# Block 1 of a two-block model on one core: wide gating products, a queued half of the output projection, key scaling on another engine, and a norm's matmul moved

## The chip, the cores and the metric

The kernel runs on one core of a Trainium2 chip. The metric is the device time of one execution in microseconds. Of the kernel before three runs are shown; their median is 2776.11 us. The engines are named as in the profile: PE is TensorE, PEld its weight loads, DVE is VectorE, ACT is ScalarE, POOL is GpSimd, SP is SyncE.

## The reference

One sequence of 512 tokens with 1024 features goes through two blocks of two layers each. The change lies in the mixers of the first block and in the norm ahead of the second. A layer of the first block is, cut to what matters:

```python
h = _rms_norm(x, in_norm_g[l])
y = h @ w_in[l] + b_in[l]
(mq, mk, mv, mo, mi, mf, hq, hf, hi, hg, sq, sk, sv) = _split_cols(y, IN_SPLITS)
qk = jax.nn.silu(_causal_conv(jnp.concatenate([mq, mk], axis=-1), ...))
m_h = mlstm_chunkwise(q, k, v, mi, mf + mlstm_f_bias[l])          # 4 heads
m_out = _head_rms_norm(m_h, mlstm_norm_g[l], 4) * sigmoid(mo)
h_h = hgrn2_chunkwise(hq, hf, hi, lb_all[l])                      # 4 heads
h_out = _head_rms_norm(h_h, hgrn_norm_g[l], 4) * silu(hg)
s_out = swa_sink_attention(q_s, k_s, v_s, swa_sinks[l])           # 8 heads
x = x + concatenate([m_out, h_out, s_out]) @ w_out[l]
u = _rms_norm(x, mlp_norm_g[l]) @ w_up[l]
x = x + square(relu(u)) @ w_down[l]
x = x + sigmoid(_rms_norm(x, ...) @ w_ple_gate[l]) * e
```

A layer of the second block first forms `mod = silu(c) @ w_mod + b_mod`, six vectors of shifts, scales and gates, and then runs three kinds of attention and a gated MLP with a short convolution. Everything is float32.

## The kernel before

The activations `x` stay in SBUF as eight tiles of 128 features by 512 tokens. Each product of float32 matrices is made of three matmuls: both factors are split into a high part (a cast on ACT, L136) and a low part (a difference on DVE, L137), and `mm3` (L176 to L178) multiplies high by high, high by low and low by high into one PSUM tile. Weights stream from HBM through SP's queue in pieces of 512 KB and are split in the same way (`wh`, `wl`). `feat_group` and `tok_group` run such products for a group of output tiles and hand each finished PSUM tile to a sink.

The mixers of a layer of block 1 are written in this order. First comes the attention with sinks (`swa`). Then `hgrn` and `mlstm`, two generators, are stepped alternately. `hgrn` goes over eight levels of a binary split of the tokens: at a level with half length h (64, 32, ... 1) it subtracts the log decays around the middle (L710, L711), takes the exponential on ACT (L715), multiplies the second halves by the queries (L718) and the first halves by the keys (L719), both on DVE and both over 128x256 elements, and runs 64x64 score matmuls (L731), whose results DVE copies into place under a mask (L742). There are two tiles a level and seven levels with products: 14 key scalings a layer. `mlstm` forms its gates and a running maximum M, sends M from POOL's queue through DRAM (L809) so that each head can read it back spread over the partitions (L850, also on POOL's queue; POOL then masks it, L852), and convolves its queries and keys on DVE (L834, L839). Each of its four heads makes four score matmuls (L858), exponentials of M on ACT (L861, L863), four products on DVE (L865), ten value matmuls (L870) and a copy to `nS` (L872).

The gates `gg` (for HGRN's output) and `gm` (for mLSTM's) come from two projections. Then follow the output projection's three parts: the attention's rows (`w_oa1`, two groups of 48 matmuls of 512 columns), HGRN's rows (`w_oh1`) and mLSTM's rows (`w_ob1`, in two halves of 256 columns). `hgrn_out` multiplies `gg` by HGRN's output and its norm factor, 16 operations of 128x64 (L779); `mlstm_out` does the same for `gm` (L896) after a norm of its own. Both are transposed on PE (L518) before their parts of the projection, and the sink adds each PSUM tile to `x` on DVE (L498).

That is the order in the source. The order in which the instructions stand on the engines is set by a scheduler, which lists all of them by priorities and a timeline of its own; the order written in the source sets the priorities. Each engine then works in order. A norm (`norm_stats`) is a list of steps that `start` begins and `tick` continues: after a number of columns of matmuls, given by the table `PAUSES` by the running number of the norm, its next step is put into the program, where the matmuls that sum the squares (L260) and the one that spreads the factor (L267) are steps. Norm 17 is that of the second half of the tokens at the entry of block 2. The eight chunks of block 1's MLP (`up`, `down`) take along the products for the second block's modulation (`mod_part`, L1034), six a chunk.

```python
    def tick(self, work):
        if self.pend:
            self.pend[0][1] += work
            if self.pend[0][1] >= self.pend[0][2]:
                self.step()
```

## Time and profile before

| what | value |
|---|---|
| median of three runs | 2776.11 us (2770.52 to 2781.68) |
| the profiled execution's own time | 2770.02 us |
| its span | 2768.2 us |
| mean granted clock of TensorE | 0.989 of full |
| busy: PE, DVE, ACT, POOL | 2691.5, 1782.7, 1182.1, 233.0 us |
| mixers of block 1, first and second layer | to about 283 us; about 703 to 985 us |
| block 2 begins | about 1430 us |

The profile is one execution. Its time is 1.8 us above its span, and it stands at the lower end of the three runs. The busy shares are means over stages with different limits, so single stretches are to be read beside them. A wait names the instruction that ended an idle time of an engine; PEclk or the last but two column of a table of stretches is the granted clock of TensorE, 1.00 for 2.4 GHz and 0.5 for 1.2 GHz.

### The profile page before, as it was taken

To read this page: it belongs to the slowest core of one execution; us is meant where nothing else is said; L and a number is where in the kernel's file an instruction comes from. 1 tells how busy PE (TensorE), PEld (TensorE's weight loads), DVE (VectorE), ACT (ScalarE), POOL (GpSimd) and SP (SyncE) were. 2 spreads that over 40 slices of the span, in tenths; PEclk is the share of its full clock that TensorE was granted. 3 is DMA by queue.
4 is the path that set the end of the run, shared out by engine and by line. 5 is a ranking of instruction groups with operands and counts; after the bars stand their busy time and mean duration, and the time that the engine had idled before them with its cause. 6 is when DMAs were issued, how large, how long until landed. Compare 5 with 4: busy or idle time off the path is not lost.

```text
span 2768.2 us, 42721 instructions
## 1 busy us (share of the span) xinstructions
PE 2691.5 (97%) x16360; PEld 2287.3 (83%) x16360; DVE 1782.7 (64%) x3888; ACT 1182.1 (43%) x2340; POOL 233.0 (8%) x606
## 2 busy tenths in 40 slices
PE   8999999999999999999999999999999999999998
PEld 7876988889977788778988777888889787888887
DVE  7677777568767767765863676655554476664555
ACT  4644532326374543233543555333234455532332
POOL 2000100002200010000122300000001310000000
PEclk9999999999999999999999999999999999999999
DMA  4211487332321127843323211233332312133222
GB/s 155 77 40 54 143 266 229 111 103 92 92 73 47 55 89 238 254 156 100 107 67 110 62 57 63 84 88 101 99 94 80 118 37 78 51 103 99 88 86 78
DMA packets 87644, 285.59 MB, mean 103 GB/s; under 512 B 10972, under 2 KB 15132, under 8 KB 87440
## 3 DMA queue, kind: packets, MB, share of 16 engines
q1 hardware_dynamic: 81280, 266.49, 30.1%
q0 software_dynamic: 5872, 16.35, 2.3%
q8 instruction: 128, 2.10, 0.3%
q14 instruction: 76, 0.62, 0.1%
q10 hardware_dynamic: 288, 0.03, 0.0%
HBM read 280.69 MB, written 2.14 MB: 102 GB/s over the span
## 4 chain that ended last, share of the span: by engine, by line
PE 80%; DVE 8%; DMA 5%; ACT 3%; issue 2%; POOL 2%; SPq 0%; DVEq 0%; ACTq 0%; POOLq 0%
PE ps_mm L176 13%; PE ps_mm L177 12%; PE ps_mm L178 12%; PE ps_T L176 5%; PE ps_T L177 5%; PE ps_T L178 5%; PE ps_S L176 5%; PE ps_S L177 5%; PE ps_S L178 5%; DMA wm<-w_mod 4%; PE ps_S L1091 2%; PE ps_o L1137 1%; DVE wm L1034 1%; PE ps_T L1131 1%; PE ps_S L582 1%
## 5 line engine op out<-in xcount | busy, mean ns | idle before, releaser
L136 ACT CAST wh<-wr 128x1024 fp32r<-128x1024 f32 (+4 forms) x414 | 406.6, 986 | 659.4 <-PE ps_mm L177 209.4
L137 DVE TENSOR_TENSOR wl<-wr,wh 128x1024 fp32r<-128x1024 f32 (+4 forms) x414 | 474.8, 1148 | 306.7 <-ACT wh L136 300.2
L176 PE MATMUL ps_mm<-slotA,wh 128*128 128x512 f32 (+1 forms) x632 | 227.1, 365 | 1.8 <-ACT slotA L317 0.7
L177 PE MATMUL ps_mm<-slotA,wh 128*128 128x512 f32 (+1 forms) x632 | 225.7, 359 | 2.0 <-DVE slotA L318 2.0
L178 PE MATMUL ps_mm<-slotA,wl 128*128 128x512 f32 (+1 forms) x632 | 224.7, 357 | 0.0
L176 PE MATMUL ps_mm<-wh,slotA 128*128 128x256 f32 (+3 forms) x688 | 207.6, 303 | 1.1 <-ACT slotB L1084 1.1
L178 PE MATMUL ps_mm<-wh,slotA 128*128 128x256 f32 (+3 forms) x688 | 205.9, 299 | 0.0
L177 PE MATMUL ps_mm<-wl,slotA 128*128 128x256 f32 (+3 forms) x688 | 205.9, 300 | 0.0
L1034 DVE CUSTOM_DVE_ANT_0 wm<-wm,sc 128x1024 f32<-128x1024 f32 x96 | 117.5, 1224 | 67.6 <-DMA wm<-w_mod 66.7
L136 ACT CAST m_h<-tmp 128x512 fp32r<-128x512 f32 (+1 forms) x122 | 71.3, 587 | 208.1 <-DVE tmp L913 171.8
L176 PE MATMUL ps_mm<-slotB,wh 128*128 128x512 f32 (+1 forms) x408 | 143.8, 357 | 3.4 <-ACT slotB L136 2.6
L176 PEld LDWEIGHTS ps_mm<-wh,slotA 128*128 128x128 f32 x688 | 131.1, 191 | 14.3 <-issue 10.6
L177 PE MATMUL ps_mm<-slotB,wh 128*128 128x512 f32 (+1 forms) x408 | 141.9, 349 | 0.0
L178 PE MATMUL ps_mm<-slotB,wl 128*128 128x512 f32 (+1 forms) x408 | 140.9, 346 | 0.0
L176 PEld LDWEIGHTS ps_mm<-slotA,wh 128*128 128x128 f32 x632 | 120.5, 193 | 21.3 <-issue 3.2
L177 PEld LDWEIGHTS ps_mm<-wl,slotA 128*128 128x128 f32 x688 | 131.1, 191 | 7.9 <-issue 6.8
L177 PEld LDWEIGHTS ps_mm<-slotA,wh 128*128 128x128 f32 x632 | 120.7, 191 | 19.8 <-DVE slotA L318 2.9
L178 PEld LDWEIGHTS ps_mm<-slotA,wl 128*128 128x128 f32 x632 | 120.8, 191 | 19.3 <-issue 3.9
L178 PEld LDWEIGHTS ps_mm<-wh,slotA 128*128 128x128 f32 x688 | 131.3, 191 | 4.5 <-issue 3.2
L1107 ACT ACTIVATE at_s<-at_s,at_st 128x512 f32<-128x512 f32 (+3 forms) x160 | 89.4, 559 | 104.0 <-DVE at_st L1105 96.2
L176 PE MATMUL ps_S<-m_h,wh 128*128 128x512 f32 (+1 forms) x355 | 129.4, 365 | 0.7 <-DVE yacc L947 0.4
L178 PE MATMUL ps_S<-m_h,wl 128*128 128x512 f32 (+1 forms) x355 | 129.2, 364 | 0.0
(633 smaller groups left out, 7183.9 us busy)
## 6 DMA issues: line engine op xcount, KB each, us to landing
wr<-w_up SPq DMA_DIRECT2D x152, 512.0 KB, 3.9
wm<-w_mod SPq DMA_DIRECT2D x96, 512.0 KB, 4.6
wr<-w_dn SPq DMA_DIRECT2D x64, 512.0 KB, 3.9
wr<-w_dn SPq DMA_DIRECT2D x32, 384.0 KB, 3.1
wr<-w_dn SPq DMA_DIRECT2D x32, 320.0 KB, 2.8
wr<-w_f SPq DMA_DIRECT2D x16, 512.0 KB, 3.7
wr<-w_pg SPq DMA_DIRECT2D x16, 512.0 KB, 3.8
wr<-w_t SPq DMA_DIRECT2D x12, 512.0 KB, 4.7
```

Of the source, the lines that this page charges most:

```text
L136: nc.scalar.copy(hi, src)
L137: nc.vector.tensor_tensor(lo, src, hi.bitcast(F32), ALU.subtract)
L176: nc.tensor.matmul(out, ah, bh, start=i == 0, stop=False)
L177: nc.tensor.matmul(out, ah, bl, start=False, stop=False)
L178: m = nc.tensor.matmul(out, al, bh, start=False, stop=i == n - 1)
L582: nc.tensor.matmul(pt, qs[f][b:b + 64, tt], qs[4][b:b + 64, k0:k0 + w], start=True, stop=True)
L1034: nc.vector.tensor_tensor_reduce(w, w, self.sc, 1.0, 0.0, ALU.mult, ALU.add, accum_out=self.mod[l][:, j:j + 1])
L1091: i = nc.tensor.matmul(pts[u], q, k, start=True, stop=True, tile_position=None if row is None else (row, 0))
L1107: nc.scalar.activation(s, s, AF.Exp, bias=st[:, 0:1], scale=-1.0, accum_out=st[:, 1:2])
L1131: nc.tensor.transpose(tp[:, c * P:c * P + P], s[:, c * P:c * P + P], self.ident)
L1137: nc.tensor.matmul(po[u * 64:u * 64 + 64], v(c, u), pT[:, c * P:c * P + P], start=c == 0, stop=c == t, tile_position=(0, u * 64))
```

## The change

Five things are done, and the source is otherwise the same.

- In `hgrn_out` the norm factor is multiplied into HGRN's output over 128x512 elements by a broadcast operand, and `gg` then takes one product of 128x256 a token tile. `mlstm_out` has the same form, with one product of 128x16x64 ahead.
- The calls of `hgrn_out` and `mlstm_out` stand ahead of the output projection.
- The second group of `w_oa1`, 48 matmuls, is issued after the last score matmul of the last mLSTM head (`issue_after`).
- HGRN's key scaling runs on POOL instead of DVE.
- Norm 17 gets longer pauses, and `mod_part` is called for one column at a time from the sink of `down`.

```diff
--- before.py
+++ after.py
@@ -28,7 +28,7 @@
 
 PAUSES = {
     5: (6000, 15000), 7: (25000, 15000), 8: (9000, 6000),
-    10: (25000, 15000), 16: (18000, 15000), 20: (6000, 15000),
+    10: (25000, 15000), 16: (18000, 15000), 17: (15000, 9000), 20: (6000, 15000),
     21: (15000, 9000), 23: (9000, 6000), 24: (6000, 15000),
 }
 
@@ -493,16 +493,17 @@
                 else:
                     nc.vector.scalar_tensor_tensor(z, th, 1.0, gh[:, 0:256], ALU.add, ALU.mult)
             self.tok_group(w, 8, 256, act, gate_sink)
+        self.hgrn_out(gg)
+        self.mlstm_out(mp, sp, gm)
 
         sub = lambda y, i: [y[t][:, i * P:i * P + P] for t in range(NT)]
         sink = lambda m, pt, sl: nc.vector.tensor_tensor(self.x[m][:, sl], self.x[m][:, sl], pt, ALU.add)
         act = [self.to_feat(X, sub(ysw, i), "mm") for i in range(4)]
         for g in range(2):
-            self.feat_group(self.wload("w_oa1", l * 2 + g, 4 * 512), 4, 4, act, sink, 4 * g)
-        self.hgrn_out(gg)
+            with self.tc.issue_after(self.done["head", 3]) if g else nullcontext():
+                self.feat_group(self.wload("w_oa1", l * 2 + g, 4 * 512), 4, 4, act, sink, 4 * g)
         act = [self.to_feat(X, sub(gg, i)) for i in range(2)]
         self.feat_group(self.wload("w_oh1", l, 2 * 1024), 2, 8, act, sink)
-        self.mlstm_out(mp, sp, gm)
         ctx.close()
         act = [self.to_feat(X, sub(gm, i)) for i in range(2)]
         wo = self.wload("w_ob1", l, 2 * 1024)
@@ -716,7 +717,7 @@
                     q4 = q_[i].rearrange("p (s two h) -> p s two h", two=2, h=h)
                     k4 = k_[i].rearrange("p (s two h) -> p s two h", two=2, h=h)
                     nc.vector.tensor_tensor(d4[:, :, 1, :], d4[:, :, 1, :], q4[:, :, 1, :], ALU.mult)
-                    nc.vector.tensor_tensor(d4[:, :, 0, :], d4[:, :, 0, :], k4[:, :, 0, :], ALU.mult)
+                    nc.gpsimd.tensor_tensor(d4[:, :, 0, :], d4[:, :, 0, :], k4[:, :, 0, :], ALU.mult)
                     ops.append((dd, dd))
                 else:
                     ops.append((k_[i], q_[i]))
@@ -773,11 +774,12 @@
 
     def hgrn_out(self, gg):
         oS, r = self.hgo
+        for u in range(2):
+            o3 = oS[u].rearrange("p (a e) -> p a e", e=64)
+            self.nc.vector.tensor_tensor(o3, o3, r[:, u * 8:u * 8 + 8].unsqueeze(2).broadcast_to([P, 8, 64]), ALU.mult)
         for t in range(NT):
-            for h in range(4):
-                g, o = gg[t][:, h * 64:h * 64 + 64], (t % 2) * 256 + h * 64
-                self.nc.vector.scalar_tensor_tensor(g, oS[t // 2][:, o:o + 64], r[:, t * 4 + h:t * 4 + h + 1], g,
-                                                    ALU.mult, ALU.mult)
+            o = (t % 2) * 256
+            self.nc.vector.tensor_tensor(gg[t], oS[t // 2][:, o:o + 256], gg[t], ALU.mult)
 
 
     def mlstm(self, l, mp, sp, yf, yv, yg, fv, fb):
@@ -855,7 +857,7 @@
                 w = S - j * P
                 js = slice(j * P, j * P + P)
                 pt = self.ps("ST"[j % 2])[:, :w]
-                nc.tensor.matmul(pt, k[b:b + 64, js], q[b:b + 64, j * P:S], start=True, stop=True)
+                self.done["head", h] = nc.tensor.matmul(pt, k[b:b + 64, js], q[b:b + 64, j * P:S], start=True, stop=True).ins
                 W = sp.tile([P, S], F32, name="ml_W", tag="ml_W", bufs=2)[:, :w]
                 aj = ac[:, j * 4 + h:j * 4 + h + 1]
                 nc.scalar.activation(W[:, 0:P], Md[:, j, :], AF.Exp, bias=aj, scale=-1.0)
@@ -890,11 +892,11 @@
         rs = sp.tile([P, 16], F32, name="ml_rs")
         self.rsqrt(sp, rs, ssq, 1.0 / 64, EPS, 16, "ml")
         nc.vector.tensor_tensor(rs, rs, r, ALU.mult)
+        n3 = num[:, :, 0:64]
+        nc.vector.tensor_tensor(n3, n3, rs.unsqueeze(2).broadcast_to([P, 16, 64]), ALU.mult)
         for t in range(NT):
-            for h in range(4):
-                g = gm[t][:, h * 64:h * 64 + 64]
-                nc.vector.scalar_tensor_tensor(g, nS[:, t, h, 0:64], rs[:, t * 4 + h:t * 4 + h + 1], g,
-                                               ALU.mult, ALU.mult)
+            g3 = gm[t].rearrange("p (h e) -> p h e", e=64)
+            nc.vector.tensor_tensor(g3, nS[:, t, :, 0:64], g3, ALU.mult)
 
 
     def mlp1(self, l, fp, act, nxt):
@@ -941,6 +943,8 @@
                 if c == 7:
                     nc.vector.tensor_tensor(self.x[m][:, sl], self.x[m][:, sl], pt, ALU.add)
                     return
+                if m < 6:
+                    self.mod_part(l, fp, c * 6 + m, c * 6 + m + 1)
                 if c == 0:
                     nc.scalar.copy(yacc[m], pt)
                 else:
@@ -960,7 +964,6 @@
         self.silu_c(fp, R2)
         for c in range(1, 8):
             up(c)
-            self.mod_part(l, fp, (c - 1) * 6, c * 6)
             down(c - 1)
         pe = []
         for k in range(2):
```

What becomes of it on the engines, in the first layer. PE at the last head of mLSTM, where L858 (now L860) are the scores, L870 (L872) the values and L176 to L178 on `slotA,wh` the matmuls of `w_oa1`. Before:

```order
L858 MATMUL ps_T<-yf_1733,yf_1801 128x384
L858 MATMUL ps_S<-yf_1733,yf_1801 128x256
L176 MATMUL ps_mm<-slotA,wh 128x512
L177 MATMUL ps_mm<-slotA,wh 128x512
L178 MATMUL ps_mm<-slotA,wl 128x512
L176 MATMUL ps_mm<-slotA,wh 128x512
L177 MATMUL ps_mm<-slotA,wh 128x512
L178 MATMUL ps_mm<-slotA,wl 128x512
L858 MATMUL ps_T<-yf_1733,yf_1801 128x128
L870 MATMUL ps_T<-yv_1522,ml_P_2466 128x66 x2
```

After the change:

```order
L872 MATMUL ps_T<-yv_1525,ml_P_2442 128x66
L860 MATMUL ps_T<-yf_1733,yf_1801 128x384
L860 MATMUL ps_S<-yf_1733,yf_1801 128x256
L860 MATMUL ps_T<-yf_1733,yf_1801 128x128
L176 MATMUL ps_mm<-slotA,wh 128x512
L177 MATMUL ps_mm<-slotA,wh 128x512
L178 MATMUL ps_mm<-slotA,wl 128x512
L176 MATMUL ps_mm<-slotA,wh 128x512
L177 MATMUL ps_mm<-slotA,wh 128x512
L178 MATMUL ps_mm<-slotA,wl 128x512
```

Before, two groups of three matmuls stood among the last head's scores and none between its values and the transposes of `gg`. Now the scores stand together, 25 matmuls of `w_oa1` follow, then that head's ten values, then 23 more, then the transposes. No matmul of `w_oa1` stands between the first three heads any more; of the 96, 70 stood ahead of the second head's first score, and now 48. In the second layer 58 stood there, and now 48.

DVE at the products for `gg` (L779, now L779 and L782; `ml_r` and `ml_ssq` belong to mLSTM's norm, `hg_t` and `hg_r` to HGRN's). Before:

```order
L130 TENSOR_TENSOR hg_t<-hg_r 128x16
L888 TENSOR_TENSOR ml_ssq<-ml_ssq,ml_r 128x16
L131 TENSOR_TENSOR hg_t<-hg_t,hg_v 128x16
L889 TENSOR_TENSOR ml_ssq<-ml_ssq,ml_r 128x16
L132 SCALAR_TENSOR_TENSOR hg_r<-hg_t,hg_r 128x16
L121 TENSOR_SCALAR ml_v<-ml_ssq 128x16
L779 SCALAR_TENSOR_TENSOR gg_1518<-slotB,hg_r,gg_1518 128x64 x4
L779 SCALAR_TENSOR_TENSOR gg_1519<-slotB,hg_r,gg_1519 128x64 x4
L779 SCALAR_TENSOR_TENSOR gg_1520<-slotB,hg_r,gg_1520 128x64 x4
L779 SCALAR_TENSOR_TENSOR gg_1521<-slotB,hg_r,gg_1521 128x64 x4
```

After the change:

```order
L882 SCALAR_TENSOR_TENSOR ml_r<-ml_nS 128x16
L779 TENSOR_TENSOR slotB<-slotB,hg_r 128x512 x2
L883 TENSOR_TENSOR ml_r<-ml_r,ml_gd 128x16
L889 TENSOR_REDUCE ml_ssq<-tmp 128x8
L782 TENSOR_TENSOR gg_1518<-slotB,gg_1518 128x256
L782 TENSOR_TENSOR gg_1519<-slotB,gg_1519 128x256
L889 TENSOR_REDUCE ml_ssq<-tmp 128x8
L782 TENSOR_TENSOR gg_1520<-slotB,gg_1520 128x256
L782 TENSOR_TENSOR gg_1521<-slotB,gg_1521 128x256
L884 RECIPROCAL ml_r<-ml_r 128x16
```

The products of `gg` stood behind mLSTM's sums of squares, in 16 pieces; now there are two wide and four of a whole tile, around those sums, with the first step on `ml_nS` ahead of them.

POOL at the transfers of M, L809 and L850 before, L811 and L852 now (L852, now L854, is the mask; `brow` and the sets to zero belong to other steps). Before:

```order
L694 MEMSET slotB 128x512 x4
L696 MEMSET slotB 128x512 x2
L402 DMA brow<-row 128x256 x2
L809 DMA ml_md_1833<-ml_Md 4x512
L850 DMA slotB<-ml_md_1833 128x512 x2
L852 AFFINE_SELECT ml_Md<-slotB 128x512
L850 DMA slotB<-ml_md_1833 128x512
L852 AFFINE_SELECT ml_Md<-slotB 128x512
```

After the change:

```order
L720 TENSOR_TENSOR tmp<-tmp,slotB 128x8x32 x2
L720 TENSOR_TENSOR tmp<-tmp,slotB 128x16x16 x2
L720 TENSOR_TENSOR tmp<-tmp,slotB 128x32x8 x2
L811 DMA ml_md_1833<-ml_Md 4x512
L720 TENSOR_TENSOR tmp<-tmp,slotB 128x64x4
L852 DMA slotB<-ml_md_1833 128x512 x2
L720 TENSOR_TENSOR tmp<-tmp,slotB 128x64x4
L854 AFFINE_SELECT ml_Md<-slotB 128x512
L720 TENSOR_TENSOR tmp<-tmp,slotB 128x128x2 x2
L720 TENSOR_TENSOR tmp<-tmp,slotB 128x256 x2
L852 DMA slotB<-ml_md_1833 128x512
L854 AFFINE_SELECT ml_Md<-slotB 128x512
```

The key scalings (L720) of the first levels stand ahead of the transfer of M, those of the levels 64x4, 128x2 and 256 between and behind its two directions. In the second layer it is the same pattern.

PE at the sums of norm 17 (L260), ahead of block 2. Before 72 matmuls of 256 columns of one projection stand ahead of them and 72 between them and L267; after the change 96 and 48. The order of SP's queue is the same before and after, as is that of all engines in block 1's MLP.

## Rows read from the trace of the kernel before

**Rows 1.** The page, part 1: busy us (share of the span) xinstructions, TensorE.

```profile
PE 2691.5 (97%) x16360; PEld 2287.3 (83%) x16360; DVE 1782.7 (64%) x3888; ACT 1182.1 (43%) x2340; POOL 233.0 (8%) x606
```

**Rows 2.** Busy time by stretch: stretch and its length, then by engine, clock, DMA.

```profile
core 0: us, PE busy (x) PEld busy (x) DVE busy (x) ACT busy (x) POOL busy (x), PEclk, DMA share, GB/s
180.00:200.00 20.00, 15.86 (x230) 14.56 (x231) 19.26 (x43) 7.24 (x10) 2.15 (x4) 1.00 0.27 81
200.00:220.00 20.00, 17.44 (x224) 14.28 (x226) 19.85 (x35) 9.12 (x14) 0.13 (x1) 0.91 0.16 54
226.00:262.00 36.00, 34.98 (x194) 25.52 (x193) 20.39 (x44) 23.02 (x56) 3.64 (x6) 1.00 0.13 45
262.30:272.80 10.50, 7.07 (x18) 4.50 (x19) 10.07 (x52) 2.12 (x4) 0.00 (x0) 0.51 0.15 50
880.00:900.00 20.00, 17.35 (x238) 16.26 (x238) 19.72 (x45) 6.79 (x10) 3.62 (x4) 0.91 0.27 81
900.00:920.00 20.00, 17.67 (x257) 14.10 (x257) 17.61 (x30) 10.60 (x19) 0.00 (x0) 0.83 0.17 55
962.00:976.00 14.00, 12.49 (x46) 8.21 (x46) 13.45 (x58) 3.66 (x6) 0.56 (x1) 0.88 0.12 40
1420.00:1440.00 20.00, 15.27 (x114) 15.02 (x113) 8.55 (x30) 7.68 (x22) 4.24 (x16) 0.91 0.08 19
```

**Rows 3.** PE's waits, 178 to 210 and 883 to 909: us, times, longest.

```profile
PE ps_o L680 <- DVE hg_st L687: 1.2, 1, 1.2
PE ps_T L814 <- DVE ml_W L807: 2.1, 1, 2.1
PE ps_o L680 <- DVE hg_st L687: 2.7, 1, 2.7
PE ps_S L731 <- DVE slotA L742: 2.0, 1, 2.0
```

**Rows 4.** PE's waits, 256 to 284.

```profile
PE ps_T L518 <- DVE gg L779: 3.7, 1, 3.7
PE ps_T L870 <- DVE ml_P L865: 0.8, 1, 0.8
```

**Rows 5.** The chain in order of time, 269 to 274: start us, us, what.

```profile
271.86 0.43 PE ps_mm L177
...
272.91 0.24 PE ps_mm L177
```

**Rows 6.** PE's waits, 1419 to 1430.

```profile
PE ps_mm L260 <- DVE n_acc L256: 4.7, 1, 4.7
```

**Rows 7.** Groups of instructions, 262 to 276: busy us, mean ns | idle before.

```profile
L896 DVE SCALAR_TENSOR_TENSOR gm<-ml_nS,ml_rs,gm 128x64 f32<-128x64 f32 x16 | 3.2, 283 | 0.0
L779 DVE SCALAR_TENSOR_TENSOR gg<-slotB,hg_r,gg 128x64 f32<-128x64 f32 x16 | 3.2, 277 | 0.0
L887 DVE TENSOR_REDUCE ml_ssq<-tmp 128x8 f32<-128x512 f32 x2 | 1.3, 654 | 0.0
```

**Rows 8.** Groups of instructions, 226 to 262.

```profile
L137 DVE TENSOR_TENSOR wl<-wr,wh 128x1024 fp32r<-128x1024 f32 x3 | 3.7, 1220 | 1.7 <-ACT wh L136 1.7
...
L176 PE MATMUL ps_mm<-slotA,wh 128*128 128x512 f32 x14 | 6.1, 433 | 0.0
```

**Rows 9.** Groups of instructions, 180 to 215.

```profile
L719 DVE TENSOR_TENSOR tmp<-tmp,slotB 128x256 f32<-128x256 f32 x7 | 2.9, 407 | 0.0
```

**Rows 10.** Lines L1069 and L1210 (duration ns min/median/max); a group of 1555 to 1562.

```profile
L1069 POOL TENSOR_TENSOR rp_a<-rp_a,rp_b x40: 725/740/1037, 1482.1 to 2275.3; 128x256 f32<-128x256 f32 x40
L1210 POOL TENSOR_TENSOR fg_b<-fg_b,c_caus x48: 448/458/1471, 1495.1 to 2224.9; 128x128 f32<-128x128 f32 x48
...
L137 DVE TENSOR_TENSOR wl<-wr,wh 128x1024 fp32r<-128x1024 f32 x2 | 2.9, 1460 | 0.4 <-ACT wh L136 0.4
```

**Rows 11.** Groups of POOL, 190 to 205.

```profile
L850 POOL DMA_DIRECT2D slotB<-ml_md x2 | 1.1, 563 | 1.9 <-PE ps_mm L178 1.9
L852 POOL TENSOR_SCALAR_AFFINE_SELECT ml_Md<-slotB 128x512 f32<-128x512 f32 x1 | 0.6, 637 | 2.9 <-DVE tmp L719 2.9
```

## The prediction

> **What bounds the kernel now.** I read the page's busy times first, then the busy times by stretch, then the waits in the stretches that stood out, then single lines. TensorE (PE) is busy 97% of the span [rows 1], so what an edit can win is PE's idle time, about 2768 − 2691.5 = 77 us in all, and the stretches in which its clock is granted at half. The reader should see in [rows 2] that around the mixers of block 1 another engine sets the pace: VectorE (DVE) is busy 19.3 and 19.9 of 20 us at 180 to 220 us (first layer), 19.7 and 17.6 at 880 to 920 (second), PE only 15.9 to 17.7. PE's waits there end on DVE each time [rows 3]: 1.2 and 2.1 us in the first layer, 2.7 and 2.0 in the second. At the end of the mixers PE waits 3.7 us for `gg`, the gated HGRN output [rows 4], and right behind it the clock is granted at 0.51 for 10.5 us [rows 2]: matmuls of 512 columns then issue every 0.43 us, and every 0.23 once the clock is back [rows 5]. In the second layer PE is busy 12.5 of 14 us at the same place, at a clock of 0.88 [rows 2]. The last place is the first norm of block 2: 4.7 us until `n_acc` [rows 6], then a clock of 0.91 over 20 us [rows 2].
>
> **Gated outputs formed ahead and wide.** Removed, per layer: 16 multiplies of 128x64 for `gg` and 16 for `gm`, 0.28 us each, which overlap to 3.2 us of busy time a group [rows 7]. Added: for `gg` two 128x512 multiplies by a broadcast factor and four of 128x256, for `gm` one of 128x16x64 and four of 128x256. No row shows the broadcast form; by the nearest, 1.22 us for a two-input operation over 1024 columns [rows 8] and 0.41 over 256 [rows 9], `gg` costs 1.22 + 4 × 0.41 = 2.9 us and `gm` the same: only 0.3 us less each. What changes is the cover. In the built order 25 matmuls of 512 columns stand behind the last head's scores, and 23 more between that head's values and the transposes of `gg`: 23 × 0.23 = 5.3 us at the full level. From the last value matmul to a complete `gg` I count 2.9 for the multiplies, 2 × 0.65 for the two sums of squares among them [rows 7], and 0.9 for a copy out of PSUM and small operations, 5.1 us in all: PE should wait 0 to 1 us where it waited 3.7; I take 0.5. Behind it DVE has the lower half of `gg`'s split behind evictions of the projection (I take 1 us of wait) and the way to `gm` (another 1 us). For the clock I keep one short fall, 0.09 of 20 us = 1.8 us, as at 200 to 220 [rows 2]. First layer: before, 3.7 + 0.8 more of idle + 10.5 × 0.49 = 9.6 us lost; after, 0.5 + 1 + 1 + 1.8 = 4.3; so −5.3 us (bounds −9.6 and 0). Second layer: before, 1.5 idle + 14 × 0.12 = 3.2; after, 1.9; so −1.3.
>
> **The other side of the queued half.** Those 48 matmuls (11 us) are taken from elsewhere: of the first layer's, 26 stood between the heads and 22 ahead of the second head. From 226 to 262 us PE was idle only 1.0 of 36 us, with DVE busy 20.4 and ACT 23.0 [rows 2]; 42 matmuls of the projection lay in it, 14 on each of three lines [rows 8], 42 × 0.23 = 9.7 us. Without them 35 − 9.7 = 25 us of PE work stand against 23 of ACT, and each head's exponentials, products and values lie bare. I charge 0.5 us a head, 2 us a layer; bounds 0 and 5 (each head by 1.2, the smallest wait of [rows 3]). Ahead of the heads, 22 × 0.23 = 5 us of matmuls fewer means that the convolution must be ready 5 us earlier. By the built order, the DVE work up to it has lost 12 (second layer: 8) key scalings of 0.41 us and some evictions, which by their rows is 5.9 us (8.1); it pays for this where those microseconds are really gone. I charge 1 us in the first layer. In the second I win back half of the 2.0 us wait of [rows 3] and half of the 3.4 us that the clock of 0.83 costs at 900 to 920 [rows 2]: −2.7.
>
> **Key scaling on GpSimd.** 28 multiplies of 0.41 us leave DVE, 11.5 us, but only those in the stretches where DVE sets the pace count: 7 at 180 to 215 us, 2.9 us [rows 9]. GpSimd (POOL) takes 0.74 for the same shape [rows 10]. And [rows 10] shows what the two engines do to each other: in 7 us of block 2 two `wl` splits of DVE take 1.46 us instead of the 1.22 of [rows 8], and POOL's 128x128 products, 0.46 in the median, up to 1.47. Here each product on POOL becomes ready together with the query product on DVE, as both wait for the same exponential. Bounds a layer: −2.9 us (all of it relief) and 7 × (0.74 − 0.41) = +2.3 (DVE stands still for all of every POOL product). I take 0, near the middle: the split beside POOL lost 0.24 us a piece, about what would be won. The Trainium skill, "SBUF — State Buffer" (🔬 SBUF: two separate sides), says that a GpSimd operation and a DVE operation with two SBUF inputs take a shared port pair as an exclusive lock for a whole instruction, so that the later one is fully blocked; by it the term would be +2.3 a layer and the sum 4.6 us higher. The trace agrees in kind, with 1.46 beside 1.22 us; nothing in it shows such pairs in a row.
>
> **Norm of block 2.** The two matmuls that sum `n_acc` move 24 matmuls of 256 columns back, 24 × 0.12 = 2.9 us (half the 0.23 of 512 columns) of the 4.7 us wait [rows 6]. 48 matmuls instead of 72 then cover the way to the diagonal's matmul, 5.8 us instead of 8.7; the 72 covered it without a wait, so up to 2.9 may be lost again. A shorter wait may spare half of the clock's 1.8 us. Bounds 0 and −4.7; I take −3, nearest to the rows moved.
>
> **The rest.** The modulation's new place in the MLP moves no instruction on any engine in the built order: 0, and the waits in the MLP stay. In the attention of block 2's first layer rows change places as a consequence: 0 ± 2.
>
> **Sum.** First layer −5.3 + 2 + 1 = −2.3; second −1.3 + 2 − 2.7 = −2.0; norm −3; the rest 0. Together −7.3 us, against the profiled 2770.0 us: 2762.7. The median of the runs stands 6.1 us higher, so as a median 2776.1 − 7.3 = 2768.8.
>
> **The rivals.** (1) *Clean.* The four waits of [rows 3] (8.0 us), both ends (9.6 + 3.2), the norm's wait (4.7) and half of the other clock losses (4) nearly vanish, 29 us, less a residue of 9: −20, 2756. For it: DVE's way gets 5.9 to 8.1 us shorter just where it sets the pace. Against: nothing covers the heads any more. (2) *The port.* DVE wins nothing from POOL, and loses 2.3 us a layer: 2768.8 + 4.6 = 2773. For it: [rows 10]. (3) *POOL's queue, the slower side.* POOL works in order, and in the built order the last levels' key scalings (64x4, 128x2, 256) stand behind the transfers of mLSTM's running maximum through DRAM. Before, POOL waited 1.9 and 2.9 us around those transfers and was busy 1.1 and 0.6 with them [rows 11], 6.5 us together. A scaling held by them holds that level's score matmuls, DVE's copy of the level and all that is behind it on DVE: up to 6.5 us and a fall of the clock of 1.8 a layer, 2 × 8.3 = 16.6 against the 7.3 won: +9, 2785. It decides where a scaling is held by more than the 2 to 3 us for which PE already waits there. Against it: the order puts products between the transfers, not all behind them. (4) *Bare heads.* 5 us a layer instead of 2: 2768.8 + 6 = 2775.
>
> **How the numbers follow.** Forecast 0.42 (2762 to 2773 as a median), clean 0.25, port or bare heads 0.20, POOL's queue 0.13. About 0.5%, 13.9 us, is what a measurement of this kernel can tell from no change. Faster by more: the clean case and the low edge of the forecast, 0.28; slower by more: the queue's case where it comes with the port, 0.11; the rest is 0.61. The range, 2747 to 2787, takes in the clean case with its residue of 9 us gone as well, and the queue's case.
>
> **What would show it.** Right: a wait for `gg` under 1 us and a clock over 0.8 at 260 to 280; shorter waits at 884 and 904; a wait for `n_acc` near 1.8; POOL products of 0.74 to 1.1. Wrong: waits of PE of over 2 us among the heads, or score matmuls of HGRN's levels that wait for POOL.

## The result, and the profile after

The change takes 2758.71 us in the median of six runs (2756.94 to 2760.22), the kernel before 2772.83 us in six runs beside it (2769.74 to 2781.68). The ratio is 0.9945, with a 95% interval from 0.9929 to 0.9961: faster by 0.55%, or by 14.1 us between the two medians. The profiled execution took 2756.94 us, 13.1 us less than that of before.

The page of the change, part 1, has PE 12 us less busy than [rows 1] and DVE within 3 us of it, though 28 products left it:

```profile
PE 2679.6 (97%) x16360; PEld 2283.1 (83%) x16360; DVE 1779.8 (65%) x3818; ACT 1182.4 (43%) x2340; POOL 258.3 (9%) x634
```

So PE's idle time hardly changed: 2755.2 − 2679.6 = 76 us, before 77. Part of what fell is the time in which PE is busy at half its clock: over the whole trace 30 us instead of 46, which is worth 8 of the 12; the other 4 are spread over matmuls at the full level, and no single row has them. The same stretches as in [rows 2] (the last one begins 8 us earlier, as all there does; columns as there):

```profile
180.00:200.00 20.00, 17.84 (x231) 16.62 (x232) 18.97 (x38) 5.98 (x9) 9.37 (x9) 0.83 0.19 54
200.00:220.00 20.00, 16.21 (x269) 13.59 (x268) 19.04 (x33) 8.76 (x13) 2.08 (x3) 0.91 0.24 81
226.00:262.00 36.00, 36.00 (x213) 29.22 (x213) 23.09 (x58) 20.36 (x50) 3.65 (x6) 1.00 0.20 60
262.30:272.80 10.50, 9.48 (x45) 7.18 (x43) 9.51 (x27) 3.13 (x4) 0.00 (x0) 1.00 0.15 51
880.00:900.00 20.00, 18.39 (x304) 17.51 (x306) 19.73 (x43) 8.14 (x13) 6.44 (x8) 0.96 0.25 81
900.00:920.00 20.00, 15.72 (x211) 12.57 (x204) 17.47 (x27) 11.74 (x23) 1.14 (x1) 0.91 0.16 54
962.00:976.00 14.00, 13.55 (x71) 11.12 (x70) 13.19 (x32) 3.18 (x4) 0.00 (x0) 1.00 0.24 75
1412.00:1432.00 20.00, 18.14 (x150) 17.88 (x149) 12.06 (x38) 9.60 (x26) 4.22 (x16) 1.00 0.08 20
```

At 262 to 273 us the clock stays at 1.00, where it was 0.51, and PE is busy 9.5 of 10.5 us. In the second layer's end it is 1.00 instead of 0.88, behind norm 17's wait 1.00 instead of 0.91. Through the heads, 226 to 262, PE does not wait at all. Two places got worse: 180 to 220 us, with the clock at 0.83 and 0.91 instead of 1.00 and 0.91, and 900 to 920 us, where PE is busy 15.7 instead of 17.7 us at a somewhat better clock. PE's waits that answer to [rows 3], [rows 4] and [rows 6], at 177 to 184, 255 to 284 and 1413 to 1430, and the three longest of eight at 874 to 913:

```profile
PE ps_o L681 <- DVE hg_st L688: 3.2, 1, 3.2
...
PE ps_mm L176 <- ACT slotA L136: 0.6, 1, 0.6
PE ps_mm L177 <- DVE slotA L137: 0.5, 1, 0.5
...
PE ps_mm L260 <- DVE n_acc L256: 1.9, 1, 1.9
...
PE ps_mm L519 <- DVE slotB L137: 1.7, 1, 1.7
PE ps_S L732 <- DVE slotA L743: 1.5, 2, 1.0
PE ps_o L681 <- DVE hg_st L686: 1.4, 1, 1.4
```

The wait for `hg_st`, HGRN's state, grew from 1.2 to 3.2 us in the first layer; that for `gg` is gone, and two of half a microsecond stand for its split; that for `n_acc` fell from 4.7 to 1.9. In the second layer the two waits of [rows 3] got shorter, 1.4 us for 2.7 and 1.5 in two pieces for 2.0, but others came beside them: the eight waits ahead of its heads make 8.3 us, where before they made 4.9.

To see where the time came from I follow the matmul that spreads a norm's factor (L267) through both traces. Its start in the two, and what the change is ahead by then:

| the norm behind | before | change | ahead by |
|---|---|---|---|
| the first layer's mixers | 306.9 | 302.5 | 4.4 us |
| its MLP, at the second layer's entry | 734.9 | 732.6 | 2.4 |
| the second layer's mixers | 1027.2 | 1021.4 | 5.8 |
| its MLP, at block 2's entry | 1409.7 | 1401.2 | 8.5 |
| norm 17 | 1436.6 | 1423.7 | 12.9 |
| last matmul of the program | 2761.1 | 2748.0 | 13.1 |

So the mixers gave 4.4 and 3.4 us, norm 17 gave 4.4, and the two MLPs, whose instructions stand in the same order in both programs, −2.0 and +2.7.

### The profile page after: what moved, and what is told of

Its sections match the earlier page's. It is cut to its first block, busy times and chain, and to the rows that moved or that the text cites. A ratio compares the mean times of both kernels' runs of the same rounds, so it can differ in the third digit from the quotient of the medians.

```text
span 2755.2 us, 42705 instructions
## 1 busy us (share of the span) xinstructions
PE 2679.6 (97%) x16360; PEld 2283.1 (83%) x16360; DVE 1779.8 (65%) x3818; ACT 1182.4 (43%) x2340; POOL 258.3 (9%) x634
## 4 chain that ended last, share of the span: by engine, by line
PE 75%; DVE 10%; DMA 8%; issue 3%; ACT 2%; POOL 2%; SPq 0%; DVEq 0%; ACTq 0%; POOLq 0%
PE ps_mm L176 12%; PE ps_mm L177 12%; PE ps_mm L178 12%; DMA wm<-w_mod 7%; PE ps_T L176 5%; PE ps_T L177 5%; PE ps_T L178 5%; PE ps_S L176 5%; PE ps_S L178 5%; PE ps_S L177 5%; PE ps_S L1094 2%; DVE wm L1037 2%; PE ps_o L1140 1%; DVE wl L137 1%; PE ps_T L1134 1%
## 5 line engine op out<-in xcount | busy, mean ns | idle before, releaser
L176 PE MATMUL ps_mm<-slotA,wh 128*128 128x512 f32 (+1 forms) x632 | 225.7, 363 | 2.8 <-ACT slotA L136 1.0
L178 PE MATMUL ps_mm<-slotA,wl 128*128 128x512 f32 (+1 forms) x632 | 224.6, 357 | 0.0
L176 PE MATMUL ps_mm<-wh,slotA 128*128 128x256 f32 (+3 forms) x688 | 207.9, 303 | 1.1 <-ACT slotB L1087 1.1
L178 PE MATMUL ps_mm<-wh,slotA 128*128 128x256 f32 (+3 forms) x688 | 206.6, 301 | 0.0
L176 PE MATMUL ps_mm<-slotB,wh 128*128 128x512 f32 (+1 forms) x408 | 142.2, 353 | 4.3 <-ACT slotB L136 3.0
L176 PEld LDWEIGHTS ps_mm<-wh,slotA 128*128 128x128 f32 x688 | 131.5, 192 | 13.3 <-issue 9.6
L178 PE MATMUL ps_mm<-slotB,wl 128*128 128x512 f32 (+1 forms) x408 | 140.6, 345 | 0.0
L176 PEld LDWEIGHTS ps_mm<-slotA,wh 128*128 128x128 f32 x632 | 119.7, 191 | 22.0 <-issue 2.0
L178 PEld LDWEIGHTS ps_mm<-wh,slotA 128*128 128x128 f32 x688 | 131.8, 192 | 5.1 <-issue 3.5
L178 PEld LDWEIGHTS ps_mm<-slotA,wl 128*128 128x128 f32 x632 | 120.4, 191 | 17.1 <-issue 2.1
L176 PE MATMUL ps_S<-m_h,wh 128*128 128x512 f32 (+1 forms) x355 | 129.5, 365 | 2.2 <-DVE yacc L951 2.0
L178 PE MATMUL ps_S<-m_h,wl 128*128 128x512 f32 (+1 forms) x355 | 129.3, 364 | 0.0
```

The source lines that it names most:

```text
L176: nc.tensor.matmul(out, ah, bh, start=i == 0, stop=False)
L178: m = nc.tensor.matmul(out, al, bh, start=False, stop=i == n - 1)
```

## The experiments

Two theories of the mixers' gain. **Relief**: a shorter DVE lets everything start earlier, and the key scaling on POOL is what shortens it. **Cover**, from the fifth kernel on sharpened to **trap**: the gain is made by the matmuls queued behind the last head, and the clock decides whether it is kept. The table has, for each kernel, the ratio to the kernel before with its interval, and from its one trace by how much the two mixers' stages and norm 17 became longer or shorter than in the trace of before (distances between the same matmuls as above). A stage in one trace is good to about 3 us: the kernel with norm 17 alone has before's order in the mixers, and its first layer took 3.2 us longer.

| kernel | ratio | 95% interval | first layer, us | second layer | norm 17 |
|---|---|---|---|---|---|
| the change | 0.9945 | 0.9929 to 0.9961 | −4.4 | −3.4 | −4.4 |
| before + norm 17 | 0.9994 | 0.9984 to 1.0004 | +3.2 | −0.8 | −1.7 |
| change, scaling on DVE | 1.0013 | 1.0004 to 1.0021 | +13.1 | −5.7 | −2.9 |
| change, no queue | 0.9999 | 0.9989 to 1.0008 | +1.3 | +1.9 | −3.2 |
| change, narrow products | 0.9955 | 0.9942 to 0.9967 | −4.6 | −6.3 | −4.4 |
| change, POOL in the first layer only | 0.9949 | 0.9935 to 0.9963 | −4.7 | −5.5 | −1.7 |
| scaling on DVE, queue behind head 3 | 0.9999 | 0.9990 to 1.0009 | +8.1 | −3.3 | −3.2 |
| before + scaling on POOL | 1.0017 | 1.0009 to 1.0026 | +3.0 | +3.4 | 0 |
| change, norm 17 later | 0.9951 | 0.9937 to 0.9965 | −5.4 | −2.2 | −2.4 |
| change, no queue, scaling on DVE | 0.9982 | 0.9973 to 0.9991 | +1.6 | −2.0 | −3.2 |
| scaling on DVE, heads after 7 steps | 1.0173 | 1.0154 to 1.0191 | +24.9 | +28.5 | −3.2 |
| scaling on DVE, heads after 6 steps | 1.0155 | 1.0138 to 1.0172 | +31.3 | +15.9 | −3.2 |
| scaling on DVE, 36 matmuls queued | 0.9956 | 0.9942 to 0.9971 | −4.9 | −5.6 | −1.7 |

Each mixers' stage can be cut in two where PE reaches the transposes of `gg`: by then it has done the same matmuls in each of these kernels, all heads and all of `w_oa1` among them. A wait for `gg` counts to the second part. Differences to before in the one trace of each, in us (minus is shorter):

| kernel | first layer: up to `gg` | from `gg` on | second layer: up to `gg` | from `gg` on |
|---|---|---|---|---|
| the change | +1.6 | −6.0 | −0.2 | −3.2 |
| change, scaling on DVE | +19.5 | −6.3 | −1.9 | −3.9 |
| change, no queue | +2.9 | −1.6 | −0.2 | +2.1 |
| change, no queue, scaling on DVE | +1.5 | +0.2 | −1.8 | −0.2 |
| before + scaling on POOL | +3.4 | −0.5 | +0.3 | +3.1 |
| scaling on DVE, 36 matmuls queued | −1.5 | −3.4 | −2.6 | −3.0 |

So what the change wins in the mixers it wins from `gg` on, and the kernels with a queue win it there with the scaling on either engine; what differs between them is the way up to `gg`.

**Norm 17 alone.**

```diff
-    10: (25000, 15000), 16: (18000, 15000), 20: (6000, 15000),
+    10: (25000, 15000), 16: (18000, 15000), 17: (15000, 9000), 20: (6000, 15000),
```

> The kernel before with the longer pauses of norm 17 alone. Theory cover (the mixers' gain comes from the matmuls queued behind the last head) and rival relief (it comes from a shorter DVE) say the same here: in the trace of the change the distance to the norm's second matmul shrank by 4.4 us at this place alone, the wait for n_acc from 4.7 to 1.9 us, with no fall of the clock behind it. So 2772.8 - 4.4 = 2768.4, ratio 0.998, and nothing else moves. If the 4.4 us were owed to the mixers' earlier end, it would be under 1.5 us.

Measured 2773.34 against 2774.47 us, a ratio whose interval reaches from 4.4 us faster to 1.1 slower. Its waits at 1425 to 1442, and its busy time from 1425:

```profile
PE ps_mm L260 <- DVE n_acc L256: 1.9, 1, 1.9
PE ps_mm L267 <- ACT n_dg L264: 1.1, 1, 1.1
...
1425.00:1445.00 20.00, 17.09 (x127) 16.63 (x126) 10.11 (x34) 8.48 (x25) 4.17 (x16) 0.91 0.07 19
```

The wait for `n_acc` is the change's 1.9 us, but here the clock falls behind it (0.91) and the diagonal's matmul waits 1.1 us more. In the change neither happened. So the expected 4.4 was one outcome of several: over the ten other kernels with these pauses, the change among them, the norm's stage got 1.7 to 4.4 us shorter. The experiment fell short of what was expected of it. In all eleven the wait for `n_acc` is 1.9 us, and two more things make the difference. The clock fell behind it in four of them, which cost 1.5 us. And the diagonal's matmul waited 1.1 us in eight: there ACT has two copies of projection tiles ahead of the diagonal (L264), in the other three, the change among them, one. Stages of 22.5, 23.7, 24.0 and 25.2 us, against 26.9 before, are neither, the wait, the fall and both; the change has neither.

**The four corners of queue and POOL.** First the change with the scaling back on DVE:

```diff
-                    nc.gpsimd.tensor_tensor(d4[:, :, 0, :], d4[:, :, 0, :], k4[:, :, 0, :], ALU.mult)
+                    nc.vector.tensor_tensor(d4[:, :, 0, :], d4[:, :, 0, :], k4[:, :, 0, :], ALU.mult)
```

> The change with HGRN's key scaling back on DVE. Theory cover: DVE got back only 11.65 - 7.8 = 3.9 us over both layers in the trace of the change, the rest went into longer subtractions and query products beside POOL; so the time stays within 2 us of the change's 2758.7. Rival relief: the key scaling is what lets the first scores start 9 and 14 us earlier; without it 5 us or more are lost, 2764 and up, with PE idle at 180 to 220 us growing.

Then without the queue, and without both:

```diff
-            with self.tc.issue_after(self.done["head", 3]) if g else nullcontext():
-                self.feat_group(self.wload("w_oa1", l * 2 + g, 4 * 512), 4, 4, act, sink, 4 * g)
+            self.feat_group(self.wload("w_oa1", l * 2 + g, 4 * 512), 4, 4, act, sink, 4 * g)
```

> The change without the queue: the second group of the attention's output projection may be issued as early as the scheduler likes. Theory cover: PE waits 2 us or more for gg in the first layer again and the clock falls behind it, +3 to +6 us, 2762 to 2765. Rival relief: gg is formed early and wide enough without it; within 1.5 us of 2758.7.

> The change with neither the queue nor the scaling on GpSimd: the early calls, the wide products and norm 17 remain. It closes a square with the change (0.9945), the one without the queue (0.9999) and the one with the scaling on DVE (1.0013). Theory trap (the queue costs where the first layer's heads begin with a wait of PE, and wins where they do not): with matmuls of 512 columns between the heads the clock stays up through them, so the queue's absence helps here: 2768 to 2772, ratio 0.998. Rival additive (each part has its own worth): 1.0013 + 0.9999 - 0.9945 = 1.0067, 2793.

And the scaling alone, put into the kernel before:

> The kernel before with the key scaling on GpSimd alone. Theory trap: worth nothing by itself, DVE gets back 4 of 11.65 us, and gg's wait at the end takes what the heads win: 2770 to 2776, the wait for gg still over 3 us. Rival relief: 5 us or more faster than before, 2767 or less.

Measured, as ratios: 0.9945 with both, 1.0013 with the queue alone, 0.9999 with POOL alone, 0.9982 with neither (the early calls, wide products and norm 17 are in all four); 1.0017 with POOL alone in the kernel before. Cover was right that the queue is needed and wrong on the scaling, relief the other way round; and three medians missed what was written for cover or trap, on the slow side: 2776.6 us against 2757 to 2761, 2772.4 against 2762 to 2765, and 2779.2 against 2770 to 2776. The two parts are each harmful by themselves, by 0.0031 and, less surely, as the intervals touch, by 0.0017, and together win 0.0037. The corner with neither came out at 0.998 as trap had it, where sums of parts would give 1.007.

Without the queue the wait for `gg` is back. PE's waits at 255 to 284 and 960 to 980 of the kernel without the queue, then at 255 to 284 of the one with neither:

```profile
PE ps_T L518 <- DVE gg L781: 4.0, 1, 4.0
...
PE ps_T L518 <- DVE gg L781: 4.3, 2, 3.6
```

```profile
PE ps_T L518 <- DVE gg L781: 4.9, 1, 4.9
```

With the queue and the scaling on DVE something else happens, in the first layer only. Its wait at 226 to 234, its busy time from 229.5 us on, and the value matmuls from 229.5 to 260:

```profile
PE ps_o L760 <- ACT slotB L765: 2.8, 1, 2.8
...
229.50:260.00 30.50, 27.92 (x102) 22.16 (x102) 10.15 (x21) 13.48 (x35) 3.11 (x5) 0.50 0.10 35
260.00:281.00 21.00, 21.00 (x87) 16.91 (x87) 13.97 (x45) 6.44 (x16) 0.56 (x1) 0.75 0.06 17
...
L872 PE MATMUL ps_T<-yv,ml_P 128*128 128x66 f32 x48 | 11.2, 425 | 0.0
```

PE waits 2.8 us for a copy of HGRN's output, the clock falls as the wait begins, and it stays at 0.50 through three heads and the scores of the fourth and is 0.75 in the 21 us from 260 on: 30.5 + 0.5 × 21 = 41 us at half. A value matmul (L872) takes 425 ns there. In the change, at 232 to 250 us, the same work runs at the full level:

```profile
L872 PE MATMUL ps_T<-yv,ml_P 128*128 128x66 f32 x60 | 7.4, 275 | 0.0
...
229.00:260.00 31.00, 31.00 (x189) 25.34 (x189) 19.12 (x50) 18.49 (x46) 3.65 (x6) 1.00 0.16 46
```

Both have the heads bare, without a matmul of the projection among them. What differs just ahead of them is the 2.8 us of wait. In the change's order the first head's scores stand 9 us earlier (209.6 us, here 218.8), ahead of HGRN's last level, and the projection's first 48 matmuls, those that are not queued, last until shortly before the first values; in this one they are used up before HGRN's output is copied. That the wait is the cause is tested below, by covering it.

**POOL in the first layer only.**

```diff
+                    (nc.gpsimd if l == 0 else nc.vector).tensor_tensor(d4[:, :, 0, :], ...)
```

> The change with the key scaling on GpSimd in the first layer and on DVE in the second. In the trace with the scaling on DVE throughout, the second layer's mixers came out 5.8 us shorter than before, in that of the change 3.4 us; the first layer lost 13.3 us, 30 us of it at half clock across the heads. Theory trap (the scaling itself is worth nothing; on DVE the first layer's heads begin with a wait of PE, the clock falls there and finds nothing dense enough to come back until the queued matmuls): this version loses nothing against the change and may win 2 us, 2755 to 2760. Rival relief (each layer gains from a shorter DVE): half of the difference between the two, +9, so about 2768.

0.9949, and the second layer came out 5.5 us shorter with the scaling on DVE there: as the trap theory has it, POOL is not needed where PE does not wait right ahead of the heads.

**Matmuls among the heads, and fewer in the queue.** With the scaling on DVE, the queue released one head earlier, then cut from 48 to 36:

```diff
-            with self.tc.issue_after(self.done["head", 3]) if g else nullcontext():
+            with self.tc.issue_after(self.done["head", 2]) if g else nullcontext():
```

> The scaling on DVE in both layers, and the queued half released after the third head's last score matmul instead of the fourth's, so that 15 to 18 matmuls of 512 columns stand between the third and the last head. Theory trap: the clock falls at the first head again (a wait of PE of 2 to 3 us at about 229), but comes back with those matmuls some 8 us after they begin, about 252 instead of 268: 4 to 7 us are won back of the 13, so 2768 to 2773. Rival relief: the clock is beside the point, what is missing is DVE time, 2774 to 2778.

```diff
+            wo = self.wload("w_oa1", l * 2 + g, 4 * 512)
+            if g:
+                self.feat_group(wo, 4, 1, act, sink, 4)
             with self.tc.issue_after(self.done["head", 3]) if g else nullcontext():
-                self.feat_group(self.wload("w_oa1", l * 2 + g, 4 * 512), 4, 4, act, sink, 4 * g)
+                self.feat_group((lambda o, c: wo(o + 1 * 512, c)) if g else wo, 4, 4 - 1 if g else 4, act, sink, 4 + 1 if g else 0)
```

> The scaling on DVE in both layers, and 36 of the 48 matmuls queued behind the last head instead of 48: 12 more stand ahead of the bare heads, where PE waited 2.9 us at 229 with all 48 queued; in the built order 25 and 11 remain behind the last head. Theory trap: that wait is covered (12 x 0.23 = 2.8 us), the clock does not fall for 30 us, the first layer comes out within 3 us of the change's and the second at least as short: 2755 to 2763. Rival relief (GpSimd's help is needed): 2766 and up, with the long fall gone or not.

Busy times of the first, from where it waits 2.8 us for the same copy, with the first released matmul, and of the second from 229 us on:

```profile
PE ps_o L760 <- ACT slotB L765: 2.8, 1, 2.8
...
230.00:247.00 17.00, 15.14 (x53) 11.77 (x54) 5.27 (x9) 8.02 (x22) 2.41 (x4) 0.51 0.20 63
247.00:257.50 10.50, 10.50 (x41) 8.41 (x39) 2.04 (x4) 3.96 (x11) 0.00 (x0) 0.50 0.00 0
257.50:260.00 2.50, 2.50 (x12) 1.97 (x11) 2.50 (x8) 0.99 (x4) 0.69 (x1) 0.99 0.00 0
...
257.87 0.50 PE L176 MATMUL ps_mm<-slotA,wh 128*128 128x512 f32 x1
```

```profile
229.00:260.00 31.00, 30.76 (x189) 24.68 (x188) 19.60 (x50) 20.70 (x52) 3.63 (x6) 1.00 0.17 53
260.00:281.00 21.00, 19.05 (x91) 14.84 (x90) 19.79 (x46) 6.20 (x10) 0.00 (x0) 0.92 0.16 52
```

Released one head earlier, the fall begins at the same wait and ends sooner, at 257.5: 27 us instead of 41, and the first layer is 5.0 us better (+8.1 against +13.1); 2772.31 us, within what was expected. But it did not come about as expected: the clock was back behind a run of scores, 0.4 us before the first of the released matmuls (257.87), so this kernel does not show that they brought it back. With 12 matmuls moved ahead of the heads the wait is gone, the clock stays at 1.00 from 229 to 260, and the time is 2761.17 us, ratio 0.9956, with every key scaling on DVE. This is the experiment that decides for trap: relief asked for 2766 and up. This kernel, too, stands near the edge: two of its twelve runs took 2774 and 2777 us at a mean clock of 0.986, the other ten 2756 to 2763 at 0.989 to 0.994; no trace shows where those two lost it.

**Heads written earlier.** Again with the scaling on DVE, and HGRN stepped seven or six times ahead of the first two heads:

```diff
-        for _ in range(9):
+        for _ in range(7):
             next(hg)
```

> The scaling on DVE and the queue, with the first two heads of mLSTM written after seven steps of HGRN instead of nine, so that in the built order the last HGRN level's 32 matmuls stand among the first heads. Theory trap: what the scaling on GpSimd really brought is the order, in which the first heads begin earlier and PE has HGRN's work where it waited 2.9 us at 229; with that here too, no fall of 30 us, the first layer within 3 us of the change's, the second better than before by 5 as with the scaling on DVE: 2755 to 2762. Rival relief: DVE lacks the 4 us that GpSimd took off it, 2766 and up.

> As the last, with six steps of HGRN ahead of the first two heads. The convolution on DVE then stands even before the seventh level: theory trap says the same range, 2753 to 2764, if PE does not wait for the convolution at the first head; rival relief 2766 and up.

Both expectations missed by far: 2821.21 and 2817.95 us. Where the first waits and its busy time at the heads, in the first and then in the second layer, and the first layer's wait for `gg`:

```profile
PE ps_S L860 <- DVE ml_P L867: 3.4, 1, 3.4
...
229.00:259.00 30.00, 30.00 (x146) 21.90 (x146) 6.16 (x13) 12.25 (x32) 3.06 (x5) 0.50 0.11 36
...
PE ps_S L860 <- DVE ml_P L867: 1.4, 1, 1.4
PE ps_T L872 <- DVE ml_P L867: 1.0, 1, 1.0
...
952.50:989.00 36.50, 36.23 (x169) 27.75 (x170) 8.38 (x18) 14.01 (x36) 2.96 (x5) 0.50 0.09 29
...
PE ps_T L519 <- DVE gg L782: 7.7, 1, 7.7
```

The wait only moved: now PE waits for the first head's own products, 3.4 us in the first layer and 1.4 and 1.0 us in the second, with the heads bare behind it, and the clock stays at 0.50 for all of the 30 and 36 us shown. In the kernel with six steps the wait is 6.4 us in the first layer, with the clock at 0.50 from 229 to 266. HGRN's rest comes last, so `gg` is 7.7 us late on top. My choice of place was wrong, and the trap is seen at its largest.

**Width, and a later norm.** The products of `gg` and `gm` in 16 pieces again, and norm 17's first pause at 20000:

```diff
...
-            self.nc.vector.tensor_tensor(gg[t], oS[t // 2][:, o:o + 256], gg[t], ALU.mult)
+            for h in range(4):
+                ...
+                self.nc.vector.scalar_tensor_tensor(g, oS[t // 2][:, o:o + 64], r[:, t * 4 + h:t * 4 + h + 1], g,
```

> The change with the products of gg and gm in 16 pieces each as before, but called ahead of the projection and with the queue. The pieces took 3.2 us of busy time a group, the wide form 3.0. Theory cover: width is worth little, within 2 us of 2758.7, since the queue hides the products. Rival width: the wide multiply by the norm factor alone can run before the gate is known and takes the chain off the end; without it gg is late by 2 us or more and the clock falls: 2762 and up.

> The change with norm 17's first pause 20000 instead of 15000: 120 matmuls ahead of its sums instead of 96, 48 behind them as in the change. The wait for n_acc, 1.9 us in the change, goes, since 24 matmuls are 2.9 us: 2757 in the median, ratio to before 0.5 to 0.7% under 1. If the way to the diagonal's matmul is longer than 48 matmuls (as where it waited 1.05 us with the clock at half), it takes back up to 1 us.

2758.9 us, ratio 0.9955: width is worth nothing that can be told. 2760.7 us, 0.9951: a later sum is not better either. Its wait for `n_acc` went, and in its place PE waits at 1410 to 1432

```profile
PE ps_mm L176 <- ACT slotA L317: 1.5, 1, 1.5
PE ps_mm L267 <- ACT n_dg L264: 1.1, 1, 1.1
```

1.1 us for the diagonal and 1.5 us for the first split activations. Neither this nor any other kernel beats the change: the next four lie between 0.9949 and 0.9956 with intervals that overlap its own.

## Why the prediction was right, and where not

The time lies inside the range, between the forecast (2762 to 2773) and the clean case (2756). The direction was right, the forecast size about half: 7.3 us, where 14 came. Point by point:

**What bounds the kernel** held: PE's waits around the mixers end on DVE, and the gain came from the ends of the mixers (−6.0 and −3.2 us from `gg` on) and from norm 17.

**Gated outputs ahead and wide**, −5.3 us: the cover was right, 23 matmuls of 0.23 us did hide the products, and the wait for `gg` went from 3.7 us to none. What was mis-sized is what would be left behind it. "For the clock I keep one short fall", 1.8 us, with 2.5 us of waits: the trace has waits of 0.6 and 0.5 us at the split, 0.5 more behind it, and no fall. The loss before was mis-read as well. In the 10.5 us at half clock PE is busy 7.07 [rows 2], and the rest is the wait for `gg` itself, so the clock cost 7.07 × 0.49 = 3.5 us and not 5.1, and the 9.6 us are 8.0. With 8.0 the term would have been −3.7; from 8.0 to 1.6 it is −6.4, and the traces differ by −6.0 from `gg` on. The two slips partly cancelled. In the second layer the end won 3.2 instead of 1.3; PE's idle time at 962 to 976 fell from 1.5 to 0.5 us and the clock there rose from 0.88 to 1.00. That the width itself adds little work or saves little was right (0.9955 with narrow products).

**The other side of the queue**, +2 a layer with bounds 0 and 5: in the change it cost nothing, PE being busy 36.00 of 36 us where it was busy 34.98, and in the second layer no wait over 0.25 us lies among the heads. But the bound was wrong in kind. I priced the bare heads by waits; their price is the clock, which once fallen ahead of them stays down: +13.1 us in the first layer with the scaling on DVE, +25 and +31 with the heads written earlier. The change stands next to this edge and did not fall over it, in all six runs, whose mean clock is 0.991 to 0.993. As far as the prediction goes that is luck: it did not weigh a wait ahead of the heads by what it does to the clock among them.

**Ahead of the heads**, +1 in the first layer: 180 to 220 us did get worse, by more. PE is busy 34.05 instead of 33.30 us there, and the clock's loss is (0.17 + 0.09) × 20 = 5.2 us instead of 1.8: +2.7, behind the 3.2 us wait for `hg_st`. All traces with POOL's scaling in the first layer have that wait, those with DVE's have 1.2 us. With the 1.0 us that the heads won, PE reaches `gg` 1.6 us later, against +3 forecast for the two together. In the second layer, where −2.7 was forecast, the waits ahead of the heads made 8.3 us instead of 4.9 and only the clock got better, 0.94 instead of 0.87 over 880 to 920; PE reaches `gg` 0.2 us earlier, against −0.7 for this and the heads together. The sign "shorter waits at 884 and 904" came true of those two and missed the ones beside them.

**Key scaling on GpSimd**, 0: mis-sized. Alone it costs 0.0017, which is 4.7 us (2.5 to 7.2), and 0.0017 again between the corners without the queue, where the intervals touch. The rival of the port named 4.6 us. DVE's operations of the levels show a part of why. In the change, the query product (L719, now beside POOL's L720) and the two subtractions (L712, L711), one line a layer, as groups over the whole span:

```profile
L719 DVE TENSOR_TENSOR tmp<-tmp,slotA 128x256 f32<-128x256 f32 x14 | 7.3, 522 | 0.0
L719 DVE TENSOR_TENSOR tmp<-tmp,slotB 128x256 f32<-128x256 f32 x14 | 6.8, 491 | 0.7 <-ACT tmp L716 0.7
L712 DVE TENSOR_TENSOR tmp<-slotB 128x256 f32<-128x256 f32 x12 | 6.6, 551 | 0.0
L712 DVE TENSOR_TENSOR tmp<-slotA 128x256 f32<-128x256 f32 x12 | 5.4, 454 | 0.0
L711 DVE TENSOR_TENSOR tmp<-slotA 128x256 f32<-128x256 f32 x12 | 5.4, 452 | 1.2 <-PE ps_T L671 0.9 <-PE ps_S L732 0.2
L711 DVE TENSOR_TENSOR tmp<-slotB 128x256 f32<-128x256 f32 x12 | 5.3, 444 | 2.4 <-PE ps_T L671 2.1 <-PE ps_S L732 0.3
...
L720 POOL TENSOR_TENSOR tmp<-tmp,slotA 128x256 f32<-128x256 f32 x14 | 13.0, 932 | 76.7 <-ACT tmp L716 76.7
L720 POOL TENSOR_TENSOR tmp<-tmp,slotB 128x256 f32<-128x256 f32 x14 | 12.9, 923 | 104.9 <-ACT tmp L716 104.9
```

and the same lines of before (L718, L711, L710) with the scaling that left (L719):

```profile
L719 DVE TENSOR_TENSOR tmp<-tmp,slotA 128x256 f32<-128x256 f32 x14 | 5.9, 419 | 0.0
L718 DVE TENSOR_TENSOR tmp<-tmp,slotA 128x256 f32<-128x256 f32 x14 | 5.9, 419 | 1.8 <-ACT tmp L715 1.8
L719 DVE TENSOR_TENSOR tmp<-tmp,slotB 128x256 f32<-128x256 f32 x14 | 5.8, 413 | 0.0
L718 DVE TENSOR_TENSOR tmp<-tmp,slotB 128x256 f32<-128x256 f32 x14 | 5.7, 410 | 0.4 <-ACT tmp L715 0.4
L710 DVE TENSOR_TENSOR tmp<-slotB 128x256 f32<-128x256 f32 x12 | 5.0, 417 | 2.2 <-PE ps_S L731 1.3 <-PE ps_T L670 0.8
L711 DVE TENSOR_TENSOR tmp<-slotB 128x256 f32<-128x256 f32 x12 | 5.0, 417 | 0.0
L710 DVE TENSOR_TENSOR tmp<-slotA 128x256 f32<-128x256 f32 x12 | 5.0, 413 | 0.6 <-PE ps_S L731 0.6
L711 DVE TENSOR_TENSOR tmp<-slotA 128x256 f32<-128x256 f32 x12 | 4.9, 410 | 0.0
```

The scaling takes 5.9 + 5.8 = 11.7 us off DVE; the query products give back 14.1 − 11.6 = 2.5, the subtractions of L712 12.0 − 9.9 = 2.1 and those of L711 10.7 − 10.0 = 0.7, and with all of DVE's instructions that grew it is 7.8. POOL needs 25.9 us for it, 0.93 a piece and not the 0.74 of [rows 10]: each side holds up the other. The Trainium skill, "SBUF — State Buffer" (🔬 SBUF: two separate sides), says that such a pair takes a shared port pair as an exclusive lock, the later one being fully blocked. The runs agree in kind, with DVE's products of 0.41 us at 0.49 and 0.52 on average beside POOL. I had weighed it against one row with 0.24 us a piece and taken the middle. That the price of 4.7 us is so near to the rival's 4.6 is not shown to have the rival's reason: DVE was to win nothing, and it kept about a third of the 11.7 us. In the trace of the scaling alone it is the clock that lost, 0.87 instead of 0.96 over 180 to 220 us, and at the second layer's end `gg` came late, with a wait of 3.2 us. What I also had wrong is where it counts: in the change, as I read its trace, the price is outweighed, as the order that the scheduler made around POOL's scaling avoids the wait ahead of the heads.

**POOL's queue**, the rival of the slower side: not seen. Of PE's waits in the mixers one ends on POOL, of 0.6 us.

**Norm of block 2**, −3: right in the wait that was moved, 2.8 us of 4.7. The trace of the change has −4.4, the other kernels with these pauses −1.7 to −4.4, and it depends on whether the clock falls behind the 1.9 us that remain (1.5 us) and on where the diagonal stands on ACT (1.1 us of wait). The prediction had allowed for both; that the change got neither is luck, and one other kernel of the ten shares it.

**The rest**, 0: right as a sum, −0.7 in the MLPs and −0.2 behind norm 17. One by one they were +2.0 and −2.7 in MLPs of the same order, which is what one trace can vary by.

**Sum**: up to `gg` +1.6 in the first layer (forecast +3) and −0.2 in the second (−0.7), from `gg` on −6.0 (−5.3) and −3.2 (−1.3), the norm −4.4 (−3), the rest −0.9 (0): −13.1 in the traces, −14.1 in the medians, against −7.3. Each term is off by less than the 3 us that a stage of one trace is good for; the size was missed because five of the six came out on the fast side, the second layer's end by most.

What stays open: why the clock fell behind the 1.9 us of the norm in four kernels and not in the other seven. That wait is the same in all, and no run here took it apart.

## What to carry to other kernels

Before filler matmuls are taken out of a stretch to cover another, look at what is left in it and at the wait ahead of it: a stretch of small matmuls that begins behind a wait can run at half clock from end to end, and that costs more than any wait in it. Here the waits were 2.8 to 6.4 us in the first layer, and 1.4 and 1.0 us in the second; how short a wait is harmless was not measured. Moving a product from DVE to GpSimd was little relief here, where the DVE's own work beside it reads two operands from SBUF: 7.8 of 11.7 us came back. Price it by a row with both engines at work. And parts of a change that go through a scheduler don't add up: test the corners before one of them is called the cause.

## What the runs showed of the hardware that was not expected

A fall of the clock at a wait of 2.8 us lasted 41 us, through three heads of mLSTM and the scores of the fourth, though PE was busy 27.9 of the first 30.5 us; it ended only among the projection's matmuls of 512 columns. With those released a head earlier it lasted 27 us, and ended behind a run of scores just before them. The same stretch entered without such a wait kept the full level for all of its 18 us. Wherever the first layer's heads were bare behind a wait of PE (2.8, 2.8, 3.4 and 6.4 us) the clock was at half for 27 to 48 us; in the five kernels with bare heads there and no wait over 0.25 us right ahead of them (the change, the one with narrow products, with POOL in the first layer only, with norm 17 later, with 36 queued) it did not fall.
